# Differential attention: one transpose turns both queries of a head, one turns both keys, and the missing halves are filled by VectorE and by transfers

## The chip, the cores and the metric

One core of a Trainium2 chip runs one kernel: a whole layer of an autoregressive decoder, batch 1, 1024 tokens, model width 1024. The metric is the device time of one execution in microseconds; the number given for a kernel is the median of several runs. A profile shows one execution of its own, engine by engine: TensorE (PE; its weight loads are PEld), VectorE (DVE), ScalarE (ACT), GpSimd (POOL) and SyncE (SP), whose queue issues most transfers. A line such as L92 is a line of the kernel file; helpers that record many instructions (L92 for matmuls, L95 for transposes, L67 for everything whose order is fixed) appear under their own line, so the tile names tell what an instruction is.

## The reference

The layer normalises its input, projects it, and runs three branches: a chunked mLSTM, a causal differential attention and a cross-attention into 256 memory tokens. The branches are projected, weighted by learned gates, added, projected again, and followed by an MLP. The part that matters here is the differential attention. It has 8 heads; each head has two queries and two keys of width 64 and one value of width 128.

```
q = rms_norm(q, q_g);  k = rms_norm(k, k_g)          # width 64, two per head
s = einsum('bhcqd,bhckd->bhcqk', qblk, kt) * d**-0.5  # c = 0, 1
s = where(kpos <= qpos, s, -inf);  p = softmax(s)
a = p[:, :, 0] - lam * p[:, :, 1]
o = rms_norm(a @ v, subln_g) * (1 - lam_init)
```

## The kernel before

The kernel keeps 32-bit precision with a faster matmul type by splitting a number into a rounded high part and a low part (the rest). A product is then three matmuls: high by high, high by low, low by high.

**Branch D** (the differential attention) is `branch_d`, with `d_gemm` as a generator for its projections. The work is cut into 16 jobs of 512 tokens: a job is one head and one half of the sequence. Each job projects four tiles of 128 tokens; a tile has eight contraction blocks of three matmuls with 384 columns (q1, q2, k1, k2 of 64 each and v of 128). So a job is 32 steps of the generator. When a tile is done, `evict` takes it out of PSUM: ScalarE and VectorE split the value, ScalarE copies the 256 q and k columns into a raw tile `draw`, each group of 64 written twice side by side, and squares them for the norm. The sums of squares are reduced on VectorE, and after the fourth tile GpSimd forms the reciprocal roots `drr`.

**Turning a job.** Scores need q and k with the 64 features on the partitions. `turns` prepares four closures per job: q1, q2, k1, k2. Each makes four TensorE transposes (one per 128 tokens) of a doubled group, so that the turned tile `pr` has the same 64 features on partitions 0 to 63 and again on 64 to 127. For a query, ScalarE writes the scaled, rounded tile over all 128 partitions and VectorE then overwrites one half with the low part. For a key, ScalarE writes the high part on all partitions (`dk`) and VectorE the low part (`dkl`). One matmul of 128 rows against `dk` then gives high by high plus low by high, and one against `dkl` adds the low part of the key. Before the keys are turned, VectorE multiplies their raw rows by the reciprocal roots (`scale`, four instructions).

**Order of the work.** The order on TensorE, VectorE and ScalarE in this branch is the order in which the program is written: `pin` and `InOrder` hold it. The main loop has 64 query steps (8 heads of 8 blocks of 128 queries) and some more to drain. A step does, in order: scores for the first query of the block; the sums of squares left over (`after`); the combination of the previous step's two softmaxes on VectorE (`combine`, tile `dpe`); four steps of the generator (`fill(4)`); the product with the values of the step before that (`values`, tile `po`); one closure from `turns`, if there is one (`p[0]`); one generator step; scores of the second query; the transposes of the combined weights (`turn`, tile `tp`, copied out to `daT`); weight conversion for the next head (`ahead`); three more generator steps, the last of which ends a tile and evicts it; then the second half of the closure (`p[1]`), which for one of the four is `scale`. A step holds eight generator steps, one tile; four steps make a job, whose closures run in the next four steps. In the following, a query step is counted within its head, 0 to 7; closures for q stand in steps 0 and 4 (and follow on). Score rows grow with the step, from one block of 128 keys to eight. Ahead of the main loop a ramp-in of eight rounds projects the first two jobs.

**Buffers.** The projection uses two PSUM banks in turn; a closure turns its rows into the bank that the tile in progress does not use (`other_tile`), so the next tile waits until that bank is read out. The transposes of the weights, the value products and the output turns share a ring of two banks. The scores have two areas of two banks. The raw tiles have a pool of seven, `dk` and `dkl` four each, `dq` two.

**Queues.** Weights come through a ring of two raw buffers by transfers that SP issues in program order; a load waits until the buffer's last conversion is done. Results of a head's half leave by a store on the same queue.

Of the kernel before, what the change touches and what calls it, by code (L numbers as in the profile page):

```python
# [10 lines left out]
F32 = mybir.dt.float32  # L11
F32R = mybir.dt.float32r
AF = mybir.ActivationFunctionType
ALU = mybir.AluOpType
# [3 lines left out]
P = 128  # L18
# [13 lines left out]
def f32(ap):  # L32
    return ap.bitcast(F32)
# [38 lines left out]
class Layer:  # L72
# [944 lines left out]
    def d_gemm(self, pool, kv):  # L1017


        nc = self.nc  # L1020
        V, A = self.V, self.A
        self.after, self.prep = [], []

        def turns(raws, rr, vh):
# [3 lines left out]
            kl = pool.tile([P, 2, 512], F32R, tag="dkl", name=self.name("dkl"))  # L1028
# [30 lines left out]
        def evict(ps, i, raws, vh, rr):  # L1059
# [6 lines left out]
            raws.append(rw)  # L1066
            vh.append(v)

            def rest():
                V.tensor_reduce(rr[:, i], scr.rearrange("p (a d) -> p a d", a=4), axis=AX.X, op=ALU.add)  # L1070
                if i == 3:
                    rl = rr.rearrange("p a b -> p (a b)")
                    self.rsqrt_mean(rl, rl, 64, 16)
                    self.prep = turns(raws, rr, vh)

            self.after.append(rest)

        for j in range(16):
            hd, hf = divmod(j, 2)
            w = self.dw[hd]  # L1080
            rr = pool.tile([P, 4, 4], F32, tag="drr", name=self.name("drr"))
            vh, raws = [], []
            for i in range(4):
                s = slice((hf * 4 + i) * P, (hf * 4 + i + 1) * P)
                ps = self.mm_tile(384)
                for k in range(NK):
                    self.mm3(ps, (self.hT[:, k, 0, s], self.hT[:, k, 1, s]), w[k], k == 0, k == NK - 1)
                    if k < NK - 1:
                        yield True
                evict(ps, i, raws, vh, rr)  # L1090
                yield True

    def branch_d(self, pool, dw):
# [705 lines left out]
    def run(self):  # L1799
        tc, nc = self.tc, self.nc  # L1800
        with ExitStack() as ctx:
            E = lambda *x, **k: ctx.enter_context(tc.tile_pool(*x, **k))
            self.cp = E(name="consts", bufs=1)
            with tc.tile_pool(name="ctmp", bufs=1) as ctmp, tc.tile_pool(name="ptc", bufs=1, space=PSUM) as self.ptp:
                self.consts(ctmp)
            c = self.cp
# [8 lines left out]
                out=self.tmaskT, in_=self.tmaskT, pattern=[[1, P]], compare_op=ALU.is_ge, fill=NEG, base=0,  # L1815
# [8 lines left out]
            with ExitStack() as c1:  # L1824
# [33 lines left out]
                with self.rings(("rpg", 2), ("ptm", 1), ("wpg", 14)) as (self.rp, ptm, self.wp):  # L1858
                    self.gwp, self.grp = self.wp, self.rp
                    dw = self.d_weights()  # L1860
                    with tc.tile_pool(name="pg", bufs=2) as self.gpool:
                        for n in range(3 * 32):
                            next(self.gates)
                            if n - 64 in (3, 7, 11, 15, 19, 23, 26, 30):
                                next(dw)
                    with tc.tile_pool(name="pd", bufs=2) as pd, tc.tile_pool(name="pd3", bufs=3) as pd3, tc.tile_pool(name="pdm", bufs=1) as pdm, tc.tile_pool(name="pd5", bufs=7) as pd5, tc.tile_pool(name="pdv", bufs=5) as pdv, tc.tile_pool(name="pdv2", bufs=17) as pdv2, tc.tile_pool(name="pd4", bufs=4) as pd4:
                        self.tmask = ptm.tile([P, D], F32, name="tmask")
                        nc.gpsimd.memset(self.tmask, 0.0)
                        nc.gpsimd.affine_select(
                            out=self.tmask[:, D - P : D], in_=self.tmask[:, D - P : D], pattern=[[-1, P]],  # L1870
                            compare_op=ALU.is_ge, fill=NEG, base=0, channel_multiplier=1,
                        )
                        class T4:
                            def tile(_, shape, dt, tag, name):
                                tag = "dscr2" if tag == "gt" else tag
                                p = pd5 if tag == "draw" else pdv if tag == "drr" else pdv2 if tag == "dv" else pd4 if tag in ("dk", "dkl") else pdm if tag == "dpe1" else pd3 if tag in ("daT", "dst") else pdm if tag in ("dscr", "dscr2", "y") else pd
# [75 lines left out]
```

## Time and profile before

| what | value |
|---|---|
| median of 3 runs | 2201.61 us (2200.49 to 2201.8) |
| the profiled execution | 2206.02 us |
| its span, first to last instruction | 2204.2 us |
| granted TensorE clock | 0.996 |
| TensorE, weight loads, VectorE, ScalarE, GpSimd busy | 99%, 85%, 63%, 44%, 24% |

Busy shares are means over a program of several stages with different limits. Matmuls are pipelined and their ends are modelled, so a TensorE that is busy 99% of the time may still be late by small amounts that only start times show. In groups and timelines a row gives the instruction's output and inputs by tile name, its shape, its length, and in brackets the idle time of its engine just before it with the engine that ended that idle time. A chain of waits is followed back from the last instruction: at each step to what released it, or to the instruction before it on its engine.

### The profile page before, as it was taken

The page shows a single profiled execution, that of the slowest core. Times are in us where ns is not written, and L with a number is a line of the kernel's source. Part 1 is how long each engine was busy: PE and PEld are TensorE (multiplying, and loading weights), DVE is VectorE, ACT ScalarE, POOL GpSimd, SP SyncE. Part 2 cuts the span into 40 slices and gives each one's busy share as a digit, 9 for nine tenths or more (in the row PEclk, how much of TensorE's full clock was granted, in tenths as well). Part 3 has the DMA queues.
Part 4 walks back from the last instruction along what each step waited for, and adds up shares of the span by engine and source line. Part 5 has one row for each costly group of instructions (what it writes and reads, how often), then busy time and mean ns, then how long its engine had stood idle before and what let it go on. Part 6 is the DMA issues. An engine that isn't in the chain of part 4 may idle for free.

```text
span 2204.2 us, 30555 instructions
## 1 busy us (share of the span) xinstructions
PE 2173.0 (99%) x11254; PEld 1878.6 (85%) x11254; DVE 1385.9 (63%) x2627; ACT 969.7 (44%) x1949; POOL 538.7 (24%) x710
## 2 busy tenths in 40 slices
PE   8999999999999999999999999999999999999998
PEld 6888789888899999999887888888878888788886
DVE  6455456554148888888752233453588778876677
ACT  7543445543246766666542121223433333443341
POOL 2210000000011111111100002102657666555544
PEclk9999999999999999999999999999999999999999
DMA  6032212202310111110144344435534454844442
GB/s 252 20 116 72 85 56 82 82 29 76 104 53 28 39 34 33 39 37 30 63 136 142 117 140 134 148 107 192 165 131 172 146 201 149 294 146 143 152 158 96
DMA packets 110947, 242.38 MB, mean 110 GB/s; under 512 B 10921, under 2 KB 19406, under 8 KB 108750
## 3 DMA queue, kind: packets, MB, share of 16 engines
q1 hardware_dynamic: 108494, 227.85, 31.4%
q10 hardware_dynamic: 2304, 12.58, 1.4%
q8 instruction: 88, 1.44, 0.3%
q14 instruction: 61, 0.50, 0.1%
HBM read 173.25 MB, written 67.14 MB: 109 GB/s over the span
## 4 chain that ended last, share of the span: by engine, by line
PE 80%; DVE 10%; ACT 4%; DMA 3%; issue 1%; POOL 0%; SPq 0%; ACTq 0%; DVEq 0%; POOLq 0%
PE mm L92 45%; PE p L92 26%; PE sc L92 4%; PE tp L95 2%; PE po L92 2%; DVE sc L67 1%; ACT dpe L67 1%; DVE dpe L67 1%; PE pr L95 1%; DVE draw L67 1%; DVE dst L67 1%; DMA xk<-in_x 0%; PE tp L92 0%; DVE drr L67 0%; ACT daT L67 0%
## 5 line engine op out<-in xcount | busy, mean ns | idle before, releaser
L92 PE MATMUL mm<-hT,w 128*128 128x512 f32 x1920 | 466.2, 396 | 3.9 <-ACT gt L601 3.9
L92 PE MATMUL mm<-w,hT 128*128 128x384 f32 (+3 forms) x2496 | 454.6, 329 | 0.0
L92 PEld LDWEIGHTS mm<-hT,w 128*128 128x128 f32 x1920 | 354.5, 189 | 78.7 <-ACT gt L601 4.8
L92 PEld LDWEIGHTS mm<-w,hT 128*128 128x128 f32 x2496 | 388.1, 188 | 8.8
L67 POOL TENSOR_TENSOR wraw<-wraw 128x128 f32<-128x128 f32 x496 | 321.8, 674 | 170.9 <-DMA wraw<-in_wdown 126.3
L92 PE MATMUL p<-xd,wo 128*128 128x512 f32 x1344 | 309.7, 393 | 6.1 <-DVE acc_xt L67 3.8
L92 PE MATMUL p<-xo,wo 128*128 128x512 f32 x1344 | 307.8, 390 | 1.8 <-DVE c L67 0.6
L92 PEld LDWEIGHTS p<-xd,wo 128*128 128x128 f32 x1344 | 254.8, 190 | 60.8 <-DVE acc_xt L67 4.2
L92 PEld LDWEIGHTS p<-xo,wo 128*128 128x128 f32 x1344 | 251.3, 188 | 57.0 <-DVE u L67 1.6
L92 PE MATMUL mm<-kt,w 128*128 128x512 f32 x1152 | 261.3, 389 | 0.0
L92 PEld LDWEIGHTS mm<-kt,w 128*128 128x128 f32 x1152 | 216.2, 188 | 44.9
L67 ACT CAST wo<-wraw 128x896 fp32r<-128x896 f32 x125 | 116.6, 944 | 264.9 <-PE p L92 111.2
L67 DVE TENSOR_TENSOR wo<-wraw,wo 128x896 fp32r<-128x896 f32 x125 | 154.2, 1241 | 117.6 <-ACT wo L67 115.9
L67 ACT ACTIVATE dpe<-sc,dst,drr 128x256 f32<-128x256 f32 (+7 forms) x128 | 106.7, 833 | 61.7 <-DVE dst L67 51.6
L116 ACT CAST w<-raw 128x256 fp32r<-128x256 f32 (+2 forms) x128 | 69.3, 566 | 134.3 <-PE mm L92 98.2
L117 DVE TENSOR_TENSOR w<-raw,w 128x256 fp32r<-128x256 f32 (+2 forms) x128 | 81.8, 663 | 49.3 <-ACT w L116 49.1
L67 DVE CUSTOM_DVE_ANT_0 sc<-sc,tmask 128x256 f32<-128x256 f32 (+7 forms) x128 | 96.8, 756 | 3.6 <-PE sc L92 2.4
L140 POOL TENSOR_SCALAR hss<-hss 128x4 f32<-128x4 f32 x8 | 3.5, 442 | 379.0 <-ACT mscr L888 379.0
L106 DVE TENSOR_TENSOR w<-raw,w 128x256 fp32r<-128x256 f32 (+1 forms) x64 | 26.6, 437 | 84.2 <-ACT w L105 83.9
L92 PE MATMUL mm<-mh,w 128*128 128x512 f32 x256 | 79.0, 389 | 0.0
L1766 POOL TENSOR_TENSOR mg<-mg,gl 128x512 f32<-128x512 f32 x16 | 20.5, 1286 | 227.7 <-DVE gl L1764 227.7
L67 DVE TENSOR_TENSOR w<-raw,w 128x384 fp32r<-128x384 f32 (+2 forms) x112 | 66.0, 599 | 15.3 <-ACT w L67 15.1
(325 smaller groups left out, 3005.8 us busy)
## 6 DMA issues: line engine op xcount, KB each, us to landing
wraw<-in_wup SPq DMA_DIRECT2D x64, 256.0 KB, 3.4
r_d<-xts SPq DMA_DIRECT2D x16, 1024.0 KB, 4.2
xd<-r_d SPq DMA_DIRECT2D x16, 1024.0 KB, 5.4
wraw<-in_wdown SPq DMA_DIRECT2D x64, 256.0 KB, 6.6
raw<-in_wgate SPq DMA_DIRECT2D x48, 256.0 KB, 3.1
gates<-gt SPq DMA_DIRECT2D x48, 256.0 KB, 2.4
raw<-in_wd SPq DMA_DIRECT2D x32, 384.0 KB, 3.2
kraw<-y SPq DMA_DIRECT2D x24, 512.0 KB, 4.3
```

The costliest lines, as they stand in the source:

```text
L67: return self.tc.keep_in_program_order(f(*a, **k))
L92: self.pin(self.nc.tensor.matmul(out, l, r, start=start, stop=stop))
L95: self.pin(self.nc.tensor.transpose(out, x, self.ident))
L106: low = lambda: self.V.tensor_sub(lo, src, f32(hi))
L116: nc.scalar.copy(hi, src)
L117: nc.vector.tensor_sub(lo, src, f32(hi))
L140: g.tensor_scalar(r, ss, 1.0 / width, EPS, op0=ALU.mult, op1=ALU.add)
L1766: G.tensor_add(mg[ft, hf], mg[ft, hf], t)
```

## The change

The raw tile of a job becomes one tile with the four groups of 64 side by side, each once. A transpose of 128 columns then turns q1 and q2 together: q1 lands on partitions 0 to 63, q2 on 64 to 127. A second one turns k1 and k2. There are eight transposes per job instead of sixteen.

For query c, ScalarE writes the high part on the half where it landed (`own[c]`), and VectorE writes the low part on the other half, reading one half of the partitions and writing the other. For key c, ScalarE writes the high part on its own half, VectorE the low part on its own half of a `kl` tile. The other half of the `kl` tile stays zero: four such tiles are kept for the whole branch and their halves are cleared once by GpSimd. The product of the low part of the query with the low part of the key thereby drops out. The other half of the high part of the key is filled by a transfer from the tile to itself, 64 partitions by 2 KB, two per job, issued on SP's queue by a third closure, `twice`. The closures per job are three instead of four; `scale` is one instruction and follows the first closure.

```diff
+        kls = [pool.tile([P, 2, 512], F32R, tag=f"dkl{i}", name=f"dkl{i}") for i in range(4)]
+        for t in kls:
+            nc.gpsimd.memset(f32(t[64:128, 0]), 0.0)
+            nc.gpsimd.memset(f32(t[0:64, 1]), 0.0)
...
             def turn(c):
                 pt = self.other_tile()
                 for i in range(4):
-                    self.transpose(pt[:, i * P : (i + 1) * P], raws[i][:, c].rearrange("p a d -> p (a d)"))
+                    self.transpose(pt[:, i * P : (i + 1) * P], rw[:, i, 2 * c : 2 * c + 2].rearrange("p a d -> p (a d)"))
                 return pt
-            def q_(c):
-                lo = slice(64 - c * 64, 128 - c * 64)
-                pt = turn(c)
-                A.activation(qT[:, c], pt, AF.Copy, scale=self.gd)
-                V.scalar_tensor_tensor(
-                    out=qT[lo, c], in0=pt[lo], scalar=self.gd[lo], in1=f32(qT[lo, c]), op0=ALU.mult, op1=ALU.subtract
-                )
+            def q_():
+                pt = turn(0)
+                for c in range(2):
+                    A.activation(qT[own[c], c], pt[own[c]], AF.Copy, scale=self.gd[own[c]])
+                for c in range(2):
+                    V.scalar_tensor_tensor(
+                        out=qT[own[1 - c], c], in0=pt[own[c]], scalar=self.gd[own[c]], in1=f32(qT[own[c], c]),
+                        op0=ALU.mult, op1=ALU.subtract,
+                    )
             def scale():
-                for i in range(4):
-                    k_ = raws[i][:, 2:4].rearrange("p c a d -> p c (a d)")
-                    V.tensor_mul(k_, k_, rr[:, i, 2:4].unsqueeze(2).broadcast_to([P, 2, P]))
-            def k_(c):
-                pt = turn(2 + c)
-                A.copy(kd[:, c], pt)
-                V.tensor_sub(kl[:, c], pt, f32(kd[:, c]))
-                if c == 1:
-                    kv.append((qT, kd, kl, vh, rr))
+                k_ = rw[:, :, 2:4]
+                V.tensor_mul(k_, k_, rr[:, :, 2:4].unsqueeze(3).broadcast_to([P, 4, 2, 64]))
+            def k_():
+                pt = turn(1)
+                for c in range(2):
+                    A.copy(kd[own[c], c], pt[own[c]])
+                for c in range(2):
+                    V.tensor_sub(kl[own[c], c], pt[own[c]], f32(kd[own[c], c]))
+            def twice():
+                for c in range(2):
+                    nc.sync.dma_start(f32(kd[own[1 - c], c]), f32(kd[own[c], c]))
+                kv.append((qT, kd, kl, vh, rr))
-            return [(lambda: q_(0), none), (lambda: q_(1), scale), (lambda: k_(0), none), (lambda: k_(1), none)]
+            return [(q_, scale), (k_, none), (twice, none)]
...
-            rw = pool.tile([P, 4, 2, 64], F32, tag="draw", name=self.name("draw"))
-            A.copy(rw, ps[:, 0:256].rearrange("p (a d) -> p a d", a=4).unsqueeze(2).broadcast_to([P, 4, 2, 64]))
+            A.copy(rw[:, i], ps[:, 0:256].rearrange("p (a d) -> p a d", a=4))
...
+            rw = pool.tile([P, 4, 4, 64], F32, tag="draw", name=self.name("draw"))
```

The pool of raw tiles goes from seven of 2 KB per partition to two of 4 KB; the four `kl` tiles take the place of the four `dkl` buffers, in another pool.

More of the change, by code (lines that the diff above doesn't have):

```diff
@@ L1022, in d_gemm, with turns @@
         self.after, self.prep = [], []
-        def turns(raws, rr, vh):
+        kls = [pool.tile([P, 2, 512], F32R, tag=f"dkl{i}", name=f"dkl{i}") for i in range(4)]
+        for t in kls:
+            nc.gpsimd.memset(f32(t[64:128, 0]), 0.0)
+            nc.gpsimd.memset(f32(t[0:64, 1]), 0.0)
+        def turns(rw, rr, vh, j):
             qT = pool.tile([P, 2, 512], F32R, tag="dq", name=self.name("dq"))
             kd = pool.tile([P, 2, 512], F32R, tag="dk", name=self.name("dk"))
-            kl = pool.tile([P, 2, 512], F32R, tag="dkl", name=self.name("dkl"))
+            kl = kls[j % 4]
+            own = (slice(0, 64), slice(64, 128))
             def turn(c):
@@ L1064, in evict @@
             scr = pool.tile([P, 256], F32, tag="dscr", name=self.name("dscr"))
             A.activation(scr, ps[:, 0:256], AF.Square)
-            raws.append(rw)
             vh.append(v)
@@ L1073, in rest @@
                     self.rsqrt_mean(rl, rl, 64, 16)
-                    self.prep = turns(raws, rr, vh)
+                    self.prep = turns(rw, rr, vh, j)
             self.after.append(rest)
@@ L1089, in d_gemm @@
                         yield True
-                evict(ps, i, raws, vh, rr)
+                evict(ps, i, rw, vh, rr, j)
                 yield True
@@ L1875, in tile @@
                                 tag = "dscr2" if tag == "gt" else tag
-                                p = pd5 if tag == "draw" else pdv if tag == "drr" else pdv2 if tag == "dv" else pd4 if tag in ("dk", "dkl") else pdm if tag == "dpe1" else pd3 if tag in ("daT", "dst") else pdm if tag in ("dscr", "dscr2", "y") else pd
+                                p = pd5 if tag == "draw" else pdv if tag == "drr" else pdv2 if tag == "dv" else pd4 if tag == "dk" else pdm if tag.startswith("dkl") else pdm if tag == "dpe1" else pd3 if tag in ("daT", "dst") else pdm if tag in ("dscr", "dscr2", "y") else pd
                                 return p.tile(shape, dt, tag=tag, name=name)
```

6 lines of the change are left out of this document (3 added, 3 removed).

## The prediction

> **What bounds the kernel now.** First the page's busy time.
>
> ```profile
> span 2204.2 us, 30555 instructions
> PE 2173.0 (99%) x11254; PEld 1878.6 (85%) x11254; DVE 1385.9 (63%) x2627; ACT 969.7 (44%) x1949; POOL 538.7 (24%) x710
> ```
>
> Over the whole span TensorE sets the time. Differential attention is one stretch, from 612 to about 1139 us; the windows view, over the ramp-in and over one whole head (eight query steps), says what it is like there (length, then busy us and instructions of TensorE, its weight loads, VectorE, ScalarE and POOL, the granted clock, the DMA share and GB/s).
>
> ```profile
> 612.00:647.00 35.00, 35.00 (x208) 34.86 (x208) 12.89 (x30) 14.42 (x34) 3.11 (x2) 1.00 0.15 42
> 776.40:835.80 59.40, 58.95 (x389) 57.13 (x388) 50.89 (x136) 40.91 (x96) 8.61 (x8) 1.00 0.13 36
> ```
>
> In the ramp-in TensorE is alone. In a head VectorE is busy 50.9 of 59.4 us, so a burst on it can reach TensorE. The chain of waits, in order of time over that head, shows where it does (start, length, what):
>
> ```profile
> 780.00 0.44 PE tp L95 x2
> ...
> 784.97 0.46 PE pr L95 x4
> ...
> 791.70 0.46 PE pr L95 x4
> ...
> 801.58 0.59 ACT daT L67
> ...
> 809.52 0.60 DVE dkl L67
> ...
> 825.56 0.66 PE tp L95 x4
> ...
> 832.36 0.46 PE pr L95 x4
> ...
> 832.84 0.70 ACT dq L67
> ...
> 833.56 0.74 DVE dq L67
> ...
> 836.13 1.34 DVE draw L67 x4
> ...
> 839.42 0.44 PE tp L95 x2
> ```
>
> The head runs from the turn (tp) at 780.00 to the same turn at 839.42. Until 801.6 TensorE paces it, from 801.6 to 825.56 VectorE and ScalarE, then TensorE until 832.8, then both others again. Of a head's eight raw-row turns (pr), four stand in stretches that TensorE paces (three of them from 784.97 on, and the one at 832.36); the others, in steps 6, 7, 0 and 2, do not stand on this chain.
>
> **The price of one turn.** In the ramp-in ScalarE's value copy marks the end of each 24-matmul tile:
>
> ```profile
> 624.54 0.27 ACT L67 CAST dv<-mm 128x128 fp32r<-128x128 f32 x1 [2.27 <-PE mm L92]
> 628.70 0.27 ACT L67 CAST dv<-mm 128x128 fp32r<-128x128 f32 x1 [2.27 <-PE mm L92]
> 633.33 0.27 ACT L67 CAST dv<-mm 128x128 fp32r<-128x128 f32 x1 [1.02 <-PE mm L92]
> ```
>
> A tile without a turn takes 628.70 - 624.54 = 4.16 us, the next, with a turn in it, 633.33 - 628.70 = 4.63 us: 0.47 us per turn of four transposes. The change removes 32 of 64 turns: 32 x 0.47 = 15.0 us of TensorE time. That is the most a purely TensorE-bound stage would give.
>
> **What is added and moved.** The q and k evictions keep their number and their width of 512 columns:
>
> ```profile
> L67 DVE SCALAR_TENSOR_TENSOR dq<-pr,dv,dq x32: 742/750/758, 631.9 to 1072.9; 64x512 fp32r<-64x512 f32 x32
> L67 ACT CAST dk<-pr x32: 580/583/588, 640.5 to 1087.2; 128x512 fp32r<-128x512 f32 x32
> L67 DVE TENSOR_TENSOR dkl<-pr,dk x32: 677/682/692, 641.1 to 1088.3; 128x512 fp32r<-128x512 f32 x32
> L67 ACT ACTIVATE dscr<-mm 128x256 f32<-128x256 f32 x64 | 25.0, 390 | 0.0
> L67 DVE TENSOR_TENSOR doS<-doS,dso 128x512 f32<-128x512 f32 x16 | 10.9, 681 | 0.0
> ```
>
> VectorE's 64-row dq takes 0.75 us, its 128-row dkl 0.68: half the rows is no cheaper. So two q and two k evictions cost what they did, but now stand two in one slot, then two in the next, then none in two steps, where before there was one in each of four. The key scaling was four instructions (1.34 us on the chain) and becomes one over 512 columns, 0.68 us by the doS row; it also moves one step earlier, from behind the second slot to behind the first. The raw copy halves its columns, 0.59 to about 0.39 us by the dscr row; ScalarE has room (40.9 of 59.4 us), so I count nothing for it. A VectorE instruction that reads one half of the partitions and writes the other has no row here. From below it could take the 64-row time, 0.75 us; from above I allow twice that, as if a read and a write passed separately. I take 0.75, the nearest row.
>
> The second thing without a row is whether VectorE may read the first half of the turned bank while ScalarE still reads the other. The nearest row is the raw copy, which needs nothing from VectorE but shares a bank with its value subtraction, in other columns:
>
> ```profile
> 796.65 0.59 ACT L67 COPY draw<-mm 128x512 f32<-128x512 f32 x1 [0.36 <-DVE dv L67]
> ```
>
> It waits for VectorE, so I take it that the two are kept apart, and VectorE's pair starts after ScalarE's pair; the other end is a start after the first. The Trainium skill, page "PSUM — Partial Sum Buffer", section "PSUM bank collisions raise a hardware error", says that two engines may not touch the same bank and 32-partition quadrant, while different quadrants are free. The row agrees for shared quadrants; for halves the rule would allow the early start, and the sum would be that of the first rival.
>
> **Ramp-in.** Between a turn and the next tile in the same bank there are 12 matmuls, 2.09 us (half of 4.16). The old pair took less. The new pairs: ScalarE starts its second some 0.1 us before the first ends (VectorE does so by 0.07 in a row below), 0.59 us after it, so q needs 0.59 + 0.69 + 0.67 + 0.75 plus about 0.4 of starts = 3.1 us, k 2.8: stalls of 1.0 and 0.7, together 1.7 against 2 x 0.47 saved there, net +0.8. At the first query step the scores are one block and the gap is still about 0.5 short: +0.5.
>
> **One head, slot by slot, in old times.** These rows are the ones moved:
>
> ```profile
> 792.20 0.69 ACT L67 ACTIVATE dq<-pr,dv 128x512 fp32r<-128x512 f32 x1
> 793.80 0.83 DVE L67 CUSTOM_DVE_ANT_0 sc<-sc,tmask 128x640 f32<-128x640 f32 x1
> 798.43 0.89 DVE L67 SCALAR_TENSOR_TENSOR dpe<-dpe,dst,dpe 128x640 f32<-128x640 f32 x1
> 800.95 0.60 PE L95 MATMUL tp<-ident,dpe 128*128 128x128 f32 x4
> 807.65 1.02 DVE L67 SCALAR_TENSOR_TENSOR dpe<-dpe,dst,dpe 128x768 f32<-128x768 f32 x1
> 808.85 0.38 PE L95 MATMUL tp<-ident,dpe 128*128 128x128 f32 x2
> ...
> 825.56 0.66 PE L95 MATMUL tp<-ident,dpe 128*128 128x128 f32 x4 [0.24 <-DVE doS L67]
> ```
>
> Step 4 (q): ScalarE's pair ends at 792.20 + 0.59 + 0.69 = 793.48, VectorE's pair takes 1.4, the score maximum starts at 794.9 instead of 793.80; with the scaling behind it the next step is 1.8 late, its combine (dpe) ends at 801.1 instead of 799.3, and the turn at 800.95 waits 0.2. Step 5 (k): the pair on ScalarE and then the pair on VectorE put the next maximum 2.1 late; the scaling that stood there is gone (1.34), so step 6 is 0.75 late, its combine ends at 809.4 and TensorE, due at 808.85, is 0.6 late. Step 7 has no turn: 0.6 - 0.47 leaves 0.13 late. VectorE has lost the dkl of steps 6 and 7 by then (2 x 0.60) and is ahead, so the 0.24 that TensorE idled ahead of step 8's turn goes: -0.1. Steps 0 and 1 have short rows and room. Step 2 is paced by VectorE: 0.70 + 0.67 + 1.34 = 2.7 before, 1.06 + 1.29 = 2.35 after, about -0.3; step 3 loses its turn, -0.47. Sum per head -0.1 - 0.3 - 0.47 = -0.9 us, of 4 x 0.47 = 1.9 removed.
>
> Against it stands a small thing that two rows show:
>
> ```profile
> 825.54 0.76 DVE L67 SCALAR_TENSOR_TENSOR dq<-pr,dv,dq 64x512 fp32r<-64x512 f32 x1
> 826.33 0.30 DVE L67 CUSTOM_DVE_ANT_0 sc<-sc,tmask 128x128 f32<-128x128 f32 x1
> 833.56 0.74 DVE L67 SCALAR_TENSOR_TENSOR dq<-pr,dv,dq 64x512 fp32r<-64x512 f32 x1 [0.42 <-ACT dq L67]
> 834.23 0.41 DVE L67 CUSTOM_DVE_ANT_0 sc<-sc,tmask 128x256 f32<-128x256 f32 x1
> ```
>
> After the dq on the upper half (825.54) the next instruction starts 0.03 us behind its end, after the one on the lower half 0.07 before it: 0.10 us for a change of half. The new order changes half about three times more per job, 0.3 us of VectorE time, of which the head as worked out feels about 0.35 in all: -0.55. The idle of 0.24 is a floor, since modelled ends of matmuls reach into it, so I take the upper part, -0.85 per head. The Trainium skill, page "VectorE: DVE Perf Modes", section "Two Vector instructions with no wait between them", has this as a rule: an instruction whose input or output starts in another quadrant than the last one's is held until VectorE is empty. The trace agrees, with that 0.10; no run here shows it for a crossing write. With the rule's price at all 0.3 us on the chain the sum would be that of the second rival.
>
> **Transfers and the rest.** Two transfers of 128 KB per job go to SP's queue, where a load may stand waiting.
>
> ```profile
> y<-yd SPq DMA_DIRECT2D x16, 256.0 KB, 2.0
> SPq L999 <- DVE w L67: 301.2, 26, 17.2
> 788.14 0.39 PE L92 MATMUL sc<-dk,dq 128*128 128x512 f32 x1
> ```
>
> A store of twice the size lands in 2.0 us. The copies are made in the job's second step and first read by the scores of its fourth: in step 1, one head ahead of 834.3, that is by 774.9, for the read at 788.14, 13 us. The queue's longest wait is 17.2 us, but SP runs ahead and such a load is released by a VectorE subtraction of the step before, ahead of the read; behind the transfer stand weight loads which themselves wait for that later subtraction. Cost nothing; without the cover each microsecond of lateness would cost 16. POOL's eight memsets (at most 0.95 each by the row here) stand in idle time:
>
> ```profile
> L1868 POOL MEMSET tmask<- x1: 953/953/953, 505.6 to 505.6; 128x1024 f32 x1
> 630.79 0.21 POOL L140 TENSOR_SCALAR drr<-drr 128x16 f32<-128x16 f32 x1 [93.33 <-DVE drr L67]
> ```
>
> They take under 8 of 93 us; uncovered they would delay the first job's scaling by that once. The matmuls against the half-zero low part keep their shapes.
>
> **Sum.** Seven heads of two jobs x -0.85 = -6.0; the last job, beside wider gate matmuls, -0.7; ramp-in +0.8; first step +0.5: -5.4 us. The profiled execution took 2206.0 us (1.8 around its span of 2204.2), so it would be 2200.6; the runs' median is 2201.6, 4.4 lower, so the forecast there is 2196.2.
>
> **Rivals.**
> 1. More than the turns. VectorE may start behind ScalarE's first half. Each pair is then about 0.6 earlier, the combines of steps 5 and 6 are in time, a head gives 1.9 and some of what it idled ahead of 825.56 and 839.42, about 2.3: 7 x 2.3 + 0.9 = 17, 2184.6. For it: the operands are disjoint halves. Against: the raw copy's wait across disjoint columns.
> 2. No change. VectorE paces more of the head than I count: the changes of half cost all their 0.3 per job on the chain and the wait of step 5 stays in TensorE's time. A head then gives 0.2 to 0.3, which the ramp-in's 1.3 nearly takes back: 2200.8. For it: VectorE's 50.9 of 59.4; against: the two emptied steps.
> 3. Slower. The crossing dq costs up to twice 0.75. Job in steps 4 to 7: 1.5 us more on the chain; in steps 0 to 3 about 1.0 us of slack absorbs part, 0.5. Seven heads x 2.0 + 1.5 in the ramp-in - 5.4 = +10: 2212. It decides from about 1.2 us per instruction. For it no row speaks; the 64-row dq shows no such surcharge with a half that stays.
> 4. The transfer doesn't hide: it stands behind a store of results, which waits for a step after the read. Some 5 us per job, +75: 2277. Against: order of issue.
>
> **Chances and range.** Forecast 0.55, rival 1 0.13, rival 2 0.22, rival 3 0.07, rival 4 0.03. The forecast's own range is 2192 to 2199. The range reaches 2186, between forecast and rival 1, and 2204, beyond no change, and leaves out some 0.17. A difference of 0.2% (4.4 us) is about what can be told from none. The forecast lies beyond it with four fifths of its chance: faster 0.44 + 0.13 = 0.57; same 0.11 + 0.20 = 0.31; slower 0.12.
>
> **What would show it.** Raw-row turns down from 256 to 128 transposes, a ramp-in with two idle gaps of TensorE ahead of a new tile; dq on VectorE near 0.75; the idle ahead of the turn in step 6 grown, that ahead of step 8's gone; a head of 58.4 to 58.8 us instead of 59.4; no wait of a score matmul on a transfer. A dq above 1.2 us, or scores waiting on a transfer, would overturn it; a head below 57.5 would speak for rival 1.

## The result and the profile after

The changed kernel takes 2206.26 us (median of 8 runs, 2204.24 to 2210.22) against 2201.73 for the kernel before in the same comparison: ratio 1.0023, 95% interval 1.0013 to 1.0033. It is slower by 4.5 us, where 5.4 fewer were forecast. A second comparison gave 1.0022 (1.0013 to 1.0031). TensorE has lost its 128 transposes (11254 instructions before, 11126 after) and 6.4 us of busy time, and the span is longer:

```profile
span 2207.6 us, 30374 instructions
PE 2166.6 (98%) x11126; PEld 1865.2 (84%) x11126; DVE 1376.0 (62%) x2579; ACT 957.6 (43%) x1949; POOL 533.6 (24%) x718
```

**Operations.** The tile views of the changed kernel (shortest/median/longest in ns, first and last start) show that no single operation is dearer than assumed: the crossing dq takes 0.751 us, as the dq that stayed on one half did before the change, the raw copy 0.37, and a transfer lands 2.2 us after its issue. In the view of waits no score matmul waits for a transfer.

```profile
L67 DVE SCALAR_TENSOR_TENSOR dq<-pr,dv,dq x32: 744/751/758, 632.9 to 1068.2; 64x512 fp32r<-64x512 f32 x32
L67 ACT COPY draw<-mm x64: 372/373/375, 617.1 to 1062.7; 128x256 f32<-128x256 f32 x64
dk<-dk SPq DMA_DIRECT2D x32, 128.0 KB, 2.2
```

**Ramp-in and first step.** In the timeline of TensorE the next tile waits for VectorE's pair on the turned bank, for 1.00, 0.68 and 0.53 us by the brackets:

```profile
634.54 2.35 PE L92 MATMUL mm<-w,hT 128*128 128x384 f32 x12 [1.00 <-DVE dq L67]
640.12 8.58 PE L92 MATMUL mm<-w,hT 128*128 128x384 f32 x48 [0.68 <-DVE dkl L67]
654.56 2.35 PE L92 MATMUL mm<-w,hT 128*128 128x384 f32 x12 [0.53 <-DVE dq L67]
```

The brackets are floors, since an idle time is counted from a modelled end. Starts show more: from the branch's first raw copy to its first output the kernel before takes 661.09 - 616.89 = 44.2 us and the changed kernel 663.86 - 617.14 = 46.7, 2.5 us more (the rows of the outputs stand further below, with more executions):

```profile
616.89 0.59 ACT L67 COPY draw<-mm 128x512 f32<-128x512 f32 x1 [0.36 <-DVE dv L67]
```

```profile
617.14 0.37 ACT L67 COPY draw<-mm 128x256 f32<-128x256 f32 x1 [0.36 <-DVE dv L67]
```

**A head.** The turn of the combined weights (tp) marks each query step. First four of them before the change (the others stand in the prediction), then the same turns after it:

```profile
786.25 0.49 PE L95 MATMUL tp<-ident,dpe 128*128 128x128 f32 x3
793.60 0.62 PE L95 MATMUL tp<-ident,dpe 128*128 128x128 f32 x4
...
817.36 0.60 PE L95 MATMUL tp<-ident,dpe 128*128 128x128 f32 x4
...
826.58 0.60 PE L95 MATMUL tp<-ident,dpe 128*128 128x128 f32 x4
```

```profile
783.54 0.44 PE L95 MATMUL tp<-ident,dpe 128*128 128x128 f32 x2 [0.46 <-DVE dpe L67]
...
789.38 0.49 PE L95 MATMUL tp<-ident,dpe 128*128 128x128 f32 x3
...
796.78 0.62 PE L95 MATMUL tp<-ident,dpe 128*128 128x128 f32 x4
...
804.33 0.66 PE L95 MATMUL tp<-ident,dpe 128*128 128x128 f32 x4
...
812.83 0.65 PE L95 MATMUL tp<-ident,dpe 128*128 128x128 f32 x4 [0.77 <-DVE dpe L67]
...
820.96 0.60 PE L95 MATMUL tp<-ident,dpe 128*128 128x128 f32 x4
...
828.77 0.62 PE L95 MATMUL tp<-ident,dpe 128*128 128x128 f32 x4
...
829.98 0.66 PE L95 MATMUL tp<-ident,dpe 128*128 128x128 f32 x4
...
842.92 0.44 PE L95 MATMUL tp<-ident,dpe 128*128 128x128 f32 x2 [0.46 <-DVE dpe L67]
```

Row by row, after minus before, with step 4 (796.78 - 793.60 = 3.18) as zero:

| turn of step | before | after | shift against step 4 | forecast |
|---|---|---|---|---|
| 4 | 793.60 | 796.78 | 0 | 0 |
| 5 | 800.95 | 804.33 | +0.20 | +0.2 |
| 6 | 808.85 | 812.83 | +0.80 | +0.6 |
| 7 | 817.36 | 820.96 | +0.42 | +0.13 |
| 0 of the next head, first turn | 825.56 | 828.77 | +0.03 | -0.1 |
| the same, second turn | 826.58 | 829.98 | +0.22 | -0.1 |
| 2 | 839.42 | 842.92 | +0.32 | -0.4 |
| 3 | 845.66 | 848.75 | -0.09 | -0.87 |

So the head is as long as before: 842.92 - 783.54 = 59.38 us against 59.42. The four turns, some 1.9 us of TensorE, have all been given back. Step 6 is 0.2 later than forecast, of which 0.1 is left at the first turn of step 0; the second turn of step 0 adds 0.2, and step 2 adds 0.4, where a gain of 0.3 was expected and a loss of 0.1 came. What takes the time are the pairs. ScalarE's and VectorE's rows for the queries (step 4) and the keys (step 1), each with the score maximum that VectorE does next:

```profile
795.38 1.38 ACT L67 ACTIVATE dq<-pr,dv 64x512 fp32r<-64x512 f32 x2
796.79 1.52 DVE L67 SCALAR_TENSOR_TENSOR dq<-pr,dv,dq 64x512 fp32r<-64x512 f32 x2 [1.12 <-ACT dq L67]
798.34 0.83 DVE L67 CUSTOM_DVE_ANT_0 sc<-sc,tmask 128x640 f32<-128x640 f32 x1
...
836.28 1.19 ACT L67 CAST dk<-pr 64x512 fp32r<-64x512 f32 x2
837.49 1.39 DVE L67 TENSOR_TENSOR dkl<-pr,dk 64x512 fp32r<-64x512 f32 x2 [0.91 <-ACT dk L67]
838.92 0.43 DVE L67 CUSTOM_DVE_ANT_0 sc<-sc,tmask 128x256 f32<-128x256 f32 x1
```

From ScalarE's start to the next maximum a query pair takes 798.34 - 795.38 = 2.96 us and a key pair 838.92 - 836.28 = 2.64. VectorE starts only behind both of ScalarE's instructions.

### The profile page after: what moved, and what is told of

Read it like the earlier page. It is cut to its first block, busy times and chain, and to the rows that moved or that the text cites. A ratio compares the mean times of both kernels' runs of the same rounds, so it can differ in the third digit from the quotient of the medians.

```text
span 2207.6 us, 30374 instructions
## 1 busy us (share of the span) xinstructions
PE 2166.6 (98%) x11126; PEld 1865.2 (84%) x11126; DVE 1376.0 (62%) x2579; ACT 957.6 (43%) x1949; POOL 533.6 (24%) x718
## 4 chain that ended last, share of the span: by engine, by line
PE 82%; DVE 8%; ACT 4%; DMA 4%; issue 2%; POOL 0%; SPq 0%; ACTq 0%; DVEq 0%; POOLq 0%
PE mm L92 46%; PE p L92 26%; PE sc L92 5%; PE tp L95 2%; PE po L92 2%; DVE sc L67 1%; ACT dpe L67 1%; DVE dkl L67 1%; PE pr L95 1%; DVE dst L67 1%; DMA kraw<-y 1%; DVE dpe L67 1%; DMA xk<-in_x 0%; ACT dk L67 0%; DMA gates<-gt 0%
## 5 line engine op out<-in xcount | busy, mean ns | idle before, releaser
L67 POOL TENSOR_TENSOR wraw<-wraw 128x128 f32<-128x128 f32 x496 | 312.7, 655 | 176.8 <-DMA wraw<-in_wdown 122.9
L92 PEld LDWEIGHTS po<-dv,daT 128*128 128x128 f32 x576 | 74.8, 189 | 0.9
```

The costliest lines, as they stand in the source:

```text
L67: return self.tc.keep_in_program_order(f(*a, **k))
L92: self.pin(self.nc.tensor.matmul(out, l, r, start=start, stop=stop))
```

## The experiments

The first kernels are the changed kernel with the edit shown; where another one is the base, the text says so. Heads are taken from the start of one head's output instruction to that of a later one, over four heads.

| kernel | us | ratio to before (95%) | head |
|---|---|---|---|
| changed kernel, again | 2207.12 | 1.0022 (1.0013 to 1.0031) | 59.39 |
| keys one step later | 2199.28 | 0.9986 (0.9977 to 0.9995) | 58.55 |
| ScalarE and VectorE in turn | 2212.51 | 1.0047 (1.0034 to 1.0059) | 60.29 |
| without transfers | 2202.76 | 1.0000 (0.9991 to 1.0009) | 59.42 |
| fixed tiles, with transfers | 2202.74 | 1.0002 (0.9993 to 1.0011) | 59.39 |
| scaling on GpSimd | 2202.59 | 1.0005 (0.9996 to 1.0014) | 58.78 |
| one low part per turn | 2183.23 | 0.9911 (0.9897 to 0.9924) | 56.95 |
| the same, low parts made twice | 2191.87 | 0.9955 (0.9939 to 0.9971) | 58.04 |
| one pair per turn | 2181.38 | 0.9904 (0.9889 to 0.9919) | 56.91 |
| one pair, fixed tiles | 2182.40 | 0.9914 (0.9900 to 0.9928) | 57.01 |
| kernel before, fixed tiles | 2198.70 | 0.9987 (0.9978 to 0.9995) | 59.51 |

**Is it the two neighbouring pairs, or the transfer?** The theory: two pairs of evictions in two neighbouring steps make VectorE late. The rival: the copies of the keys by transfer cost. The first kernel scales and turns the keys one step later, and so issues the transfers later too.

```diff
-            return [(q_, scale), (k_, none), (twice, none)]
+            return [(q_, none), (lambda: None, scale), (k_, none), (twice, none)]
```

> The changed kernel with its keys turned and evicted one step later, in step 2 or 6 of a head instead of 1 or 5; the scaling one step later too. Burst theory: the turn of step 6 no longer waits 0.77 us for its combine, and the bank wait of 0.29 ahead of step 2's tile goes; another wait may come in step 3 or 7. A head falls from 59.4 to about 58.7 us, the time from 2206.3 to about 2201. Transfer theory (the added transfers cost the time): nothing changes, 2206 within 1.5.

Measured: head 58.55, 2199.3. The head is 0.8 shorter and the time is below that of the kernel before. The second kernel has no transfers: the other half of each key tile stays zero, which leaves out the product of the low part of the query with the high part of the key.

```diff
-                for c in range(2):
-                    nc.sync.dma_start(f32(kd[own[1 - c], c]), f32(kd[own[c], c]))
```

> The changed kernel without the 32 transfers: the other half of each high key tile stays zero, so the product of the low part of the query with the high part of the key is left out; matmuls and evictions are the same. Burst theory: 2206 within 1.5. Transfer theory: back to 2202 or below.

Measured: head 59.42, so the transfers cost a head nothing; but 2202.8 instead of 2206. That kernel also keeps the keys' high parts in four fixed tiles, in another pool, so the next two separate the transfers from the place of the tiles.

> The changed kernel once more, beside the next three. If the transfers (or where the tiles lie) cost something outside the heads, it comes out at 2206.3 again, 3.5 above the kernel without transfers (2202.8). If that difference was only the spread between two measurements, it comes out near 2203 to 2204. The head should be 59.4 us in both cases.

> The keys' high parts lie in four fixed tiles, as in the kernel without transfers, but the transfers are made. If the transfers cost the 3.5 us: 2206, as the changed kernel. If where the tiles lie makes the difference: 2202.8, as the kernel without transfers. The head is 59.4 us in both, since no score waits for a transfer.

The changed kernel comes out at 2207.1 again, so the difference is not a spread between two measurements. With the transfers and fixed tiles (`kds[j % 4]` in place of a rotating tile) it is 2202.7, with fixed tiles and without transfers 2202.8. So the transfers cost nothing, and the place of the tiles is worth 4.4 us. What that is, the section on place shows.

**Are the two engines kept apart over the whole bank?**

```diff
                 for c in range(2):
                     A.copy(kd[own[c], c], pt[own[c]])
-                for c in range(2):
                     V.tensor_sub(kl[own[c], c], pt[own[c]], f32(kd[own[c], c]))
```

(and so for the queries).

> The changed kernel with each pair in the order ScalarE, VectorE, ScalarE, VectorE. If ScalarE and VectorE are kept apart over a whole bank, the second ScalarE copy now waits for the first subtraction and ScalarE's queue behind it is late: 2207 to 2215. If they are kept apart only on the same half, the first subtraction starts 0.7 us earlier and the time falls to 2200 or less. The transfer theory expects 2206 either way.

Measured: head 60.29, 2212.5. In the timeline of this kernel ScalarE's second half waits for VectorE to finish reading the first, 0.81 us; its next instruction, the output copy yd, comes late by as much, and TensorE's turn behind it waits 0.85:

```profile
828.33 0.68 ACT L67 ACTIVATE dq<-pr,dv 64x512 fp32r<-64x512 f32 x1
829.82 0.68 ACT L67 ACTIVATE dq<-pr,dv 64x512 fp32r<-64x512 f32 x1 [0.81 <-DVE dq L67]
```

```profile
831.27 0.66 PE L95 MATMUL tp<-ident,dpe 128*128 128x128 f32 x4 [0.85 <-ACT yd L67]
```

ScalarE and VectorE are kept apart in this program also where they work on different halves of a bank. Whether the order is kept by the bank or by the tile that both also touch (dq, dk), these kernels don't tell; the raw copy shown in the prediction shares only the bank. What the chip would do without that wait was not tried.

**What in the pair costs: the count of instructions, or the halves?** In the next kernel ScalarE copies the whole turned tile twice (128 rows), VectorE makes one low part of 128 rows, and transfers bring the query's low halves to their places; both keys share one low tile, and no half is kept zero, which adds a product of two low parts.

```diff
                 for c in range(2):
-                    A.activation(qT[own[c], c], pt[own[c]], AF.Copy, scale=self.gd[own[c]])
+                    A.activation(qT[:, c], pt, AF.Copy, scale=self.gd)
...
+                V.scalar_tensor_tensor(out=lo, in0=pt, scalar=self.gd, in1=f32(qT[:, 0]), op0=ALU.mult, op1=ALU.subtract)
...
+                    nc.sync.dma_start(f32(qT[own[1 - c], c]), f32(lo[own[c]]))
...
-                    A.copy(kd[own[c], c], pt[own[c]])
...
-                    V.tensor_sub(kl[own[c], c], pt[own[c]], f32(kd[own[c], c]))
+                    A.copy(kd[:, c], pt)
+                V.tensor_sub(kl, pt, f32(kd[:, 0]))
```

> The changed kernel with one VectorE instruction per turn over all 128 partitions instead of two over 64: ScalarE writes the high parts twice over all partitions, VectorE one tile with both low parts, and transfers move the low parts of the queries to the other half (four transfers per job in all instead of two). Both keys share one low tile, which adds a product of low parts of the other query. Burst theory: VectorE's part of a slot falls from 1.5 and 1.4 us to 0.75 and 0.69, the combines of steps 5 and 6 are in time, a head falls to about 57.6 us and the time to 2190 to 2195. Transfer theory: twice the transfers, 2206 to 2212.

Measured: 2183.2, better than expected; the head gives 59.41 - 56.95 = 2.46 us, more than the four turns, since the idle TensorE had before is gone too. The counterpart takes this kernel and makes each low part twice, the second time into a tile that nobody reads:

```diff
+                for o in (lo, self.lo2):
-                V.scalar_tensor_tensor(out=lo, in0=pt, scalar=self.gd, in1=f32(qT[:, 0]), op0=ALU.mult, op1=ALU.subtract)
+                    V.scalar_tensor_tensor(out=o, in0=pt, scalar=self.gd, in1=f32(qT[:, 0]), op0=ALU.mult, op1=ALU.subtract)
...
+                for o in (kl, self.lo2):
-                V.tensor_sub(kl, pt, f32(kd[:, 0]))
+                    V.tensor_sub(o, pt, f32(kd[:, 0]))
```

> The kernel with one low part per turn (2183.2, head 56.95), but VectorE makes each low part twice, over all 128 rows, the second into a tile that nobody reads: as many VectorE instructions of the same length as in the changed kernel, without a change of half and without a wait between two halves of a bank. If the amount of VectorE's work in two neighbouring steps is what the changed kernel pays for: most of the 2.4 us per head come back, 58.8 to 59.3, and the whole 2199 to 2204. If it is the changes of half and the crossing writes: head 57.2 or less, 2186.

Measured: head 58.04, 2191.9: between the two. Timeline rows of the kernel with low parts made twice, and then of the kernel with one:

```profile
790.12 1.27 ACT L67 ACTIVATE dq<-pr,dv 128x512 fp32r<-128x512 f32 x2
791.42 0.75 DVE L67 SCALAR_TENSOR_TENSOR dql<-pr,dv,dq 128x512 fp32r<-128x512 f32 x1 [1.00 <-ACT dq L67]
792.09 0.74 DVE L67 SCALAR_TENSOR_TENSOR dlo<-pr,dv,dq 128x512 fp32r<-128x512 f32 x1
792.75 0.82 DVE L67 CUSTOM_DVE_ANT_0 sc<-sc,tmask 128x640 f32<-128x640 f32 x1
...
798.45 1.07 ACT L67 CAST dk<-pr 128x512 fp32r<-128x512 f32 x2
...
799.56 0.69 DVE L67 TENSOR_TENSOR dkl<-pr,dk 128x512 fp32r<-128x512 f32 x1 [0.61 <-ACT dk L67]
800.16 0.68 DVE L67 TENSOR_TENSOR dlo<-pr,dk 128x512 fp32r<-128x512 f32 x1
800.76 0.96 DVE L67 CUSTOM_DVE_ANT_0 sc<-sc,tmask 128x768 f32<-128x768 f32 x1
```

```profile
784.82 1.26 ACT L67 ACTIVATE dq<-pr,dv 128x512 fp32r<-128x512 f32 x2
...
786.78 0.82 DVE L67 CUSTOM_DVE_ANT_0 sc<-sc,tmask 128x640 f32<-128x640 f32 x1
...
792.55 1.08 ACT L67 CAST dk<-pr 128x512 fp32r<-128x512 f32 x2
...
794.26 0.96 DVE L67 CUSTOM_DVE_ANT_0 sc<-sc,tmask 128x768 f32<-128x768 f32 x1
```

| from ScalarE's start to the next maximum | queries | keys | head |
|---|---|---|---|
| halves, two low parts (changed kernel) | 2.96 | 2.64 | 59.39 |
| whole tiles, low parts made twice | 792.75 - 790.12 = 2.63 | 800.76 - 798.45 = 2.31 | 58.04 |
| whole tiles, one low part | 786.78 - 784.82 = 1.96 | 794.26 - 792.55 = 1.71 | 56.95 |

The same number of instructions, over whole tiles instead of halves, is shorter by 0.33 us per pair: some 0.1 on ScalarE (1.38 and 1.19 against 1.27 and 1.07), the rest on VectorE. A head has four pairs: 4 x 0.33 = 1.3 us, and the head is 59.39 - 58.04 = 1.35 shorter. From turn to turn of the weights the same two timelines show where:

| to the turn of step | halves (changed kernel) | whole tiles, low parts made twice | gain |
|---|---|---|---|
| 5, from 4 | 804.33 - 796.78 = 7.55 | 798.88 - 791.54 = 7.34 | 0.21 |
| 6, from 5 | 812.83 - 804.33 = 8.50 | 806.85 - 798.88 = 7.97 | 0.53 |
| 0, second, from the first | 829.98 - 828.77 = 1.21 | 823.80 - 822.82 = 0.98 | 0.23 |
| 2, from 1 | 842.92 - 836.84 = 6.08 | 836.36 - 830.66 = 5.70 | 0.38 |

All other intervals agree within 0.02. So the gain stands at the turns behind the pairs. The key pairs read and write the same half in the changed kernel and gain the same 0.33 as the crossing query pairs, so the crossing is not what costs. The two kernels also differ by two transfers per job; the changed kernel's own transfers cost nothing.

The second low part takes 0.67 and 0.60, 2.5 us per head, of which the head shows 1.09: with it gone TensorE paces, and only one wait on the combine, 0.3 us of a weight load, is left between 640 and 1050 us.

The scaling of the keys is a third part of VectorE's work beside the pairs. Here the changed kernel is the base again:

```diff
-                V.tensor_mul(k_, k_, rr[:, :, 2:4].unsqueeze(3).broadcast_to([P, 4, 2, 64]))
+                nc.gpsimd.tensor_mul(k_, k_, rr[:, :, 2:4].unsqueeze(3).broadcast_to([P, 4, 2, 64]))
```

> The changed kernel with the scaling of the keys on GpSimd, which has idle time: VectorE loses one instruction of 0.68 us per job, right behind its pair for the queries. If VectorE's burst of work is what makes the combines late: the wait of step 5 (0.24) and that of step 2 (0.24) go, step 6's (0.97) falls by 0.5 to 0.7, so a head is about 1.1 us shorter, 58.3, and the whole 2206.3 - 8 = 2198. If the serial order of ScalarE's pair and VectorE's pair is what counts, and not the amount of VectorE's work: head 59.4, 2206. If GpSimd's scaling isn't done by the turn of the keys one step later (7 us), the turn waits and the head is longer than 59.4.

Measured: head 58.78, 2202.6. This lies between the two that were expected. The wait of step 5 (0.21 us, of a weight load) went; that of step 6 fell from 0.77 to 0.38, by 0.39 where 0.5 to 0.7 was expected; step 2 kept its 0.46 where it was expected to go, as it follows the key pair, not the scaling:

```profile
780.89 0.44 PE L95 MATMUL tp<-ident,dpe 128*128 128x128 f32 x2 [0.47 <-DVE dpe L67]
809.57 0.66 PE L95 MATMUL tp<-ident,dpe 128*128 128x128 f32 x4 [0.38 <-DVE dpe L67]
```

So the amount of VectorE's work counts, but 0.21 + 0.39 = 0.6 us per head is all that the scaling is worth.

**A pair of one and one.** The base is the kernel with one low part, but ScalarE reads the bank once; the second high copy is made by GpSimd from SBUF.

```diff
-                for c in range(2):
-                    A.copy(kd[:, c], pt)
+                A.copy(kd[:, 0], pt)
                 V.tensor_sub(kl, pt, f32(kd[:, 0]))
+                nc.gpsimd.tensor_copy(kd[own[1], 1], f32(kd[own[1], 0]))
```

(and so for the queries).

> As the kernel with one low part per turn (2183.2, head 56.95), but the bank is read by one ScalarE and one VectorE instruction only; the second high copy (64 rows) is made by GpSimd from SBUF. ScalarE loses 0.6 to 0.7 us per turn, and VectorE starts that much earlier. If VectorE's lateness still cost TensorE something there (some 0.3 us of waits are left in a head, and 0.3 in the ramp-in), a head is 56.6 to 56.9 and the whole 2180 to 2182. If TensorE is already the only bound, 2183. If GpSimd's copies come late (they are followed by the transfers and read two steps later) or slow VectorE down, above 2184.

Measured: 2181.4, ratio 0.9904, the fastest here, though its interval overlaps that of the kernel with one low part. The head hardly moved (56.91). The windows view of one head (TensorE busy first) shows why: TensorE is busy for all of it, and no VectorE or ScalarE time that is taken away there can show.

```profile
776.40:833.31 56.91, 56.91 (x374) 55.52 (x373) 47.21 (x127) 37.25 (x93) 11.08 (x12) 1.00 0.22 56
```

**The place of the tiles.** Behind the branch the next pass starts with loads. In the windows view, TensorE's busy time in the 60 us from the branch's last output is 57.70 before, 56.74 in the changed kernel, and 60.00 with fixed tiles and transfers (the number behind the instruction count is the granted clock; the changed kernel's second profile has 57.82 at a clock of 1.00, so the lower clock is not what makes the idle time):

```profile
1138.72:1198.72 60.00, 57.70 (x249) 0.97 0.62 202
```

```profile
1141.61:1201.61 60.00, 56.74 (x244) 0.97 0.62 193
```

```profile
1140.87:1200.87 60.00, 60.00 (x267) 1.00 0.62 206
```

In the first two SP's queue holds a load of that pass until the last value products are done (po), for 3.4 us, though not the same load in both (first the kernel before, then the changed one); in the two kernels with fixed tiles, with transfers and without, the view has no such wait:

```profile
SPq L1688 <- PE po L92: 3.4, 1, 3.4
SPq L150 <- PE po L92: 3.4, 1, 3.4
```

> The kernel before, with the keys' high and low parts in four fixed tiles each instead of a rotating pool; no instruction is changed. If the 3.5 to 4.4 us between the changed kernel and the two kernels with fixed tiles come from where the tiles lie (behind the stage a load then needn't wait for the last value products, and TensorE's idle of 2.3 us there goes): 2202 - 4 = 2198, with a head of 59.41. If they come from something in the changed kernel only: 2202.

> The kernel whose turned bank is read by one ScalarE and one VectorE instruction (2181.4), with the keys' parts in fixed tiles. If the place of the tiles is worth 3.5 to 4.4 us in every kernel: 2177 to 2178, with the same head (56.91). If not: 2181.

Fixed tiles take 3.3 us off the kernel before too (2198.7), with no idle TensorE in those 60 us. They take nothing off the fastest kernel (2182.4 against 2181.4), which had only 0.8 us of idle there; its idle went and the time did not. And in the kernel before with fixed tiles a wait for the last value products is still there, at another load (3.3 us), without idle TensorE. So where the tiles lie decides whether TensorE idles behind the branch, in the old kernel as in the new; by which load or wait is not shown.

**Where the 4.5 us are.** The head is unchanged, and up to the first output 2.5 us are lost. For the rest more executions of both kernels were profiled.

> The kernel before once more, for a second profile of it. The execution profiled first lies 4.3 us above its own median; the changed kernel's two profiles are 2.2 us above it on average, the medians of the runs 4.5 to 5.1. If the missing 2 to 3 us are the spread of one execution, this profile has the same head (59.41) and the same 477.6 us from the first query step's output to the last, and a shorter start of the stage or a shorter rest of the kernel behind it (1065.5 in the first profile).

> A third profile of the kernel before. From the first query step's output to the last 477.6 us again; from there to the end 1062.3 and 1065.5 in the first two profiles. If behind the stage nothing differs between the kernels, the mean over the profiles is the same for both, near 1064 to 1065.

> A third profile of the changed kernel. 2.34 us of idle TensorE in the ramp-in and 477.8 us from the first query step's output to the last, as in the first two; behind the stage 1066.0 and 1064.9 there. If part of the 4.5 to 5.1 us lies behind the stage, its mean there stays 1.5 us or more above that of the kernel before.

> A fourth profile of the kernel before, for the same comparison: 477.6 us within the stage, 2.3 us of idle TensorE right behind it.

> A fourth profile of the changed kernel, for the same comparison: 477.8 us within the stage, 2.2 to 3.3 us of idle TensorE right behind it.

The first row of each kernel's first profile is that of the branch's first output, the second that of its last:

```profile
661.09 0.35 ACT L67 ACTIVATE doS<-po,dst 128x128 f32<-128x128 f32 x1
1138.72 0.37 ACT L67 ACTIVATE doS<-po,dst 128x128 f32<-128x128 f32 x1 [3.49 <-PE po L92]
```

```profile
663.86 0.36 ACT L67 ACTIVATE doS<-po,dst 128x128 f32<-128x128 f32 x1
1141.61 0.37 ACT L67 ACTIVATE doS<-po,dst 128x128 f32<-128x128 f32 x1 [3.49 <-PE po L92]
```

| four profiles each | first raw copy to first output | first to last output | from there to the end of the span |
|---|---|---|---|
| before | 44.2, 44.2, 44.2, 44.2 | 477.6, 477.6, 477.3, 477.4 | 1065.5, 1062.3, 1063.7, 1064.0 |
| changed | 46.7, 46.7, 46.7, 46.7 | 477.8, 477.9, 477.8, 477.9 | 1066.0, 1064.9, 1065.0, 1061.3 |
| difference of the means | +2.5 | +0.35 | +0.4 |

Inside the branch the profiles of one kernel agree within 0.3 us, and the change costs 2.8 to 2.9 us there. Between the outputs the first head is 1.0 us longer (59.98 against 59.02), the five in the middle are level, and the rest is about half a microsecond shorter. Behind the branch nothing can be told from the spread of 3 to 5 us between executions of one kernel; the 1.5 us that would have spoken for a loss there did not come. So the branch shows 2.8 of the 4.5 to 5.1 us, at the lower ends of the two intervals (2.9). With the key tiles fixed in both kernels (ratios 0.9987 and 1.0002, each within 0.0009) the change costs 3.3 us, and the branch shows 2.2 of it. The last 1 to 2 us stay open: no stage shows them.

## Why the prediction was wrong, by its own steps

- **Price of a turn, number of turns:** right. 32 turns are gone, and where TensorE paces, a head's busy time falls by 58.95 - 56.91 = 2.04 us (kernel with one pair), about 0.5 for each of its four turns.
- **Evictions keep their price, the crossing dq at 0.75:** right, 0.751. The rival of a crossing write at twice the price is out: the kernel is slower, but not by that.
- **VectorE starts behind both of ScalarE's instructions:** right. The rival of an early start is out: the changed kernel shows VectorE held behind ScalarE's other half, the interleaved one ScalarE behind VectorE's.
- **Ramp-in and first step, +0.8 and +0.5:** the waits are the ones forecast, 1.00, 0.68 and 0.53 by the brackets, but the cost is too low: 2.5 us up to the first output instead of 1.3. The forecast's figures agree with the brackets, which are floors. The first head behind it is 1.0 longer than before, which was in no term.
- **Transfers and memsets cost nothing:** right. With fixed tiles the kernel takes 2202.74 us with the transfers and 2202.76 without; the eight memsets are over by 558.7, long before the first turn at 630.8.
- **Steps 4 to 8 of a head:** the mechanism was right, with the 0.2 of step 5. Step 6 came 0.80 late instead of 0.6, and the second turn of step 8 (step 0 of the next head) was not in the sum at all: its weight load waits 0.38 for the output copy yd, which ScalarE does behind the longer query pair.
- **Step 2, 2.7 to 2.35, -0.3:** wrong in size. The 2.35 was the pair of evictions of the keys; it measures 2.64. Its turn moved by +0.10 against that of step 0.
- **"A small thing", changes of half:** this is the term that failed. I counted 0.3 us per job, let the head feel 0.35 of it, and then took nearly nothing: -0.85 out of -0.9. The kernel that makes its low parts twice has the same count of instructions without halves; its pairs are 0.33 shorter and its head 1.35. The price of one change held: on VectorE 0.67 and 0.60 from start to start become 0.75 and 0.69. But the two pairs of a job are 0.66 longer by it, not 0.3. Two things were left out. ScalarE too does not overlap two instructions on different halves: its pairs take 1.38 and 1.19, where whole tiles take 1.27 and 1.07. And I let the head feel about half of the cost, when the turns of steps 5, 6, 0 and 2 feel all of it, 1.35.
- **The rest of the head, -0.9 without changes of half:** too low as well. That same kernel, with the same count of instructions, gives 59.41 - 58.04 = 1.37. So the head is -1.37 + 1.35, where -0.9 + 0.05 was forecast: two errors, of which the second was the larger.
- **Sum:** the heads were to give 6.0 us and gave about nothing; ahead of the first output 2.5 were lost instead of 1.3. The second rival, no change because the changes of half cost all they can and step 5's wait stays, came nearest in mechanism, with 2200.8, 0.8 faster than before. Against it the branch shows 2.8 slower, 3.6 us apart: 1.2 ahead of the first output, and 2.4 behind it, where seven heads were to give 0.3 each. The measured 4.5 holds 1 to 2 us more, which stay open.

The "changes of half" are on VectorE what the Trainium skill, page "VectorE: DVE Perf Modes", section "Two Vector instructions with no wait between them", states of quadrants: an instruction that starts in another one than the last is held until the engine is empty. The changed kernel's pairs agree. The crossing dq pair takes 1.52 us for two instructions of 0.75, none of it overlapped, where the kernel with low parts made twice starts the second 0.67 us after the first (792.09 - 791.42), before that one's 0.75 are over. For the keys, which stay on their half, it is 1.39 for two of 0.69 against a start 0.60 after the first (800.16 - 799.56).

## What to carry to other kernels

Half of the partitions is not half an instruction: a 64-row copy cost the 128-row time here, so cutting an eviction into halves doubles its engine time, and each change of half added some 0.1 us to it on both engines. Where an operation merges on one engine, see that it merges on the engines that empty its result; here one low part over all 128 rows, with transfers for the halves, turned a loss of 4.5 us into a gain of 20. And when removed work is paid for in a stage of small slack, follow the pair from its first start to the next instruction behind it, for every pair: 0.33 us there, four times a head, was more than the whole gain that was forecast. And compare a change that also moves tiles with the old kernel at the same places: that alone was worth 3.3 and 4.4 us in two kernels here, and nothing in a third.

## What the runs showed of the hardware that was not expected

ScalarE starts a second whole-tile copy 0.5 us after the first (two in 1.08 us, each 0.58 to 0.59), but a second copy on the other half only 0.6 after it (1.19): it too loses its overlap of 0.1 us at a change of half. GpSimd copies 64x512 from SBUF in 0.62 us (a row of the kernel with one pair) and scales 128x512 in 1.05, against 0.68 on VectorE (tile view of the kernel with the scaling on GpSimd):

```profile
792.54 0.62 POOL L1054 CAST dk<-dk 64x512 fp32r<-64x512 f32 x1 [6.24 <-ACT dk L67]
```

```profile
L1053 POOL TENSOR_TENSOR draw<-draw,drr x16: 1046/1050/1052, 632.9 to 1061.5; 128x512 f32<-128x512 f32 x16
```

And the kernel before, with no instruction changed, was 3.3 us faster with some of its tiles in other places.
